# A two-block transformer kernel in split f32: weights one unit ahead, norm casts in pairs, transposes turned later, modulation steps spread

## The chip, the cores and the metric

The kernel runs on one core of one Trainium2 chip. The metric is the device time of one execution in microseconds (us); lower is better. TensorE is called PE here, VectorE DVE, ScalarE ACT, GpSimd POOL, and SyncE SP (the engine that issues the weight loads). Each engine runs its instructions in a fixed order; a scheduler sets that order when the program is built, and semaphores hold an instruction until its inputs are there.

## The reference, cut to what matters

256 tokens of width 1024 pass through a first block and then two layers of a second one. All is f32.

```python
def first_block(x, ...):                       # DEPTH = 1
    xn = rmsnorm(h, norm1_g); proj = xn @ w_in          # weights "wp"
    h = h + concat([moba_attention(...), hgrn2(...)]) @ w_out   # "wo"
    hn = rmsnorm(h, norm2_g)
    h = h + peer(hn, wq, subkeys, u, v)                  # "wq", "pu", "pv"
    return rmsnorm(h, normf_g)

def one(xb):                                   # peer: 16384 experts, 8 heads
    s = einsum(xb @ wq, subkeys)               # scores of two halves of a key
    v1, i1 = top_k(s[:, :, 0], 16); v2, i2 = top_k(s[:, :, 1], 16)
    sc, p = top_k(v1[..., :, None] + v2[..., None, :], 16)
    eidx = take_along_axis(i1 * 128 + i2, p)   # places of the chosen experts
    act = gelu(einsum(xb, u[eidx]))
    return einsum(softmax(sc) * act, v[eidx])

def even_layer(x, c, ...):                     # layer 0; layer 1 has attention instead
    sh_m, sc_m, g_m, sh_f, sc_f, g_f = split(silu(c) @ ada_w + ada_b, 6)
    h = modulate(rms_norm(x, mix_norm), sh_m, sc_m)
    y = mixer(h @ w_in) @ w_out                # "wi0", "wo0"   (layer 1: "wi1", "wo1")
    x = x + g_m * y
    hf = modulate(rms_norm(x, ffn_norm), sh_f, sc_f)
    return x + g_f * ((silu(hf @ w_gate) * (hf @ w_up)) @ w_down)   # "fgu", "fd"
```

## The kernel before, in words

**Products.** Every f32 product is done as three products of a high and a low part: hi by hi, hi by lo, lo by hi. The high part is a cast (on ACT), the low part a subtraction (on DVE). For weights these are `hi` (L193) and `lo` (L194); for a few units of "wq" and "pu" POOL does the subtraction. The matmuls are L224, L225 and L228 where the weights stand still in the array (128x256 results, "wq" and "pu" mainly), and L252, L253 and L254 where the activations stand still (128x512 results).

**The stream of weights.** All weights come in one order, in units of two halves; a half is 128x1024 f32, 512 KB, loaded into one of four `raw` buffers by SP and turned into `hi` and `lo` by ACT and DVE. There are three buffer pairs for `hi` and `lo`, and five more in the stretches where memory has room (`roomy`). `unit()` hands out a unit and first calls `load()` for those ahead of it: one unit, two where there is room. The place of a `load()` in the program sets where its cast and its subtraction stand in the orders of ACT and DVE.

**The norm.** `norm_t` runs before "wp", "wq", "wi0", "fgu0", "wi1" and "fgu1". For each half `t` of the tokens DVE forms the scale of the rows (L397 to `dr`, L409), PE turns the rows and scales them (L417, eight blocks of 128 columns), ACT scales each block (`y`, L420), casts four blocks at a time (`xh`, L424), DVE subtracts (`xl`, L425). Then PE starts the next product (`ahead`). The residual sum of the stage before is part of it (`gy` L744, `h` L745).

**PEER.** `places(t)` works out on DVE where each chosen expert lies (L876 to L878 per head group and half, results `res`), turns three tables on PE (L882) and copies them out (`idxT`, L883). `steps()` runs it in pieces beside the products with "pu"; `due` says beside which half. The tables are used by `gate4` (masks `A` L932 and `B` L933, product L935) from half 40 of "pu" on.

**Modulation.** `ada_steps` forms the six modulation vectors of a layer from 48 rows of `ada_w` (each 512 KB, `araw`): one DVE instruction per row (L1071), a sum at the end of a vector (L1075), and for the two gates a turn on PE (L1052), a copy on ACT (L1054) and a 4 KB store by SP (`send`). Layer 0's steps run beside "pv", layer 1's beside "fgu0" and "fd0".

**The feed-forward part.** `ffn` has 11 blocks of "fgu": 48 matmuls, then silu on ACT (L1110) and a product on DVE (`fy`, L1111), and a turn on PE (L1103) that is deferred into the next block, behind its k = 2.

Of the kernel before, what the change touches and what calls it, by code (L numbers as in the profile page):

```python
# [137 lines left out]
class Prog:  # L138
# [61 lines left out]
    def unit(self, nm, j):  # L200
        n = self.pos[(nm, j)]
        while self.nload < len(self.order) and self.nload <= n + (2 if self.roomy(self.nload) else 1):
            self.load(self.nload)
            self.nload += 1
        return self.ready.pop(n)
# [75 lines left out]
    def out_n512(self, nm, j0, x, first=None, step=None):  # L281

        us, acc = first or ([], [[self.acc([128, 512])], None])
        acc[1] = [self.acc([128, 512])]
        for k in range(8):
            if k // 4 == len(us):
                us.append(self.unit(nm, j0 + k // 4))
            o = (k % 2) * 512
            for t in (1,) if first else (0, 1):
                ins = self.xstat(acc, us[k // 4][k // 2 % 2], x, k, k == 0, k == 7, [(0, slice(o, o + 512))], ts=(t,))  # L290
            if k == 2:
                self.pump(ins)
            if step:
                step()
        return acc[0][0], acc[1][0]

    def ahead(self, nm, j0, x):

        us = [self.ready.pop(self.pos[(nm, j0 + n)]) for n in range(2)]
        acc = [[self.acc([128, 512])], None]  # L300
        for k in range(8):
            o = (k % 2) * 512
            ins = self.xstat(acc, us[k // 4][k // 2 % 2], x, k, k == 0, k == 7, [(0, slice(o, o + 512))], ts=(0,))
            if k == 5:
                self.mark = ins.ins
        return us, acc
# [65 lines left out]
    def norm_t(self, pool, side, nm, gain, shift=None, row=None):  # L372
# [7 lines left out]
        with self.tc.tile_pool(name="nrm", bufs=1, side=side) as tp:  # L380
            for t in range(2):
# [29 lines left out]
                for g in range(2):  # L411
# [6 lines left out]
                    for k in range(4):  # L418
# [3 lines left out]
                                             **({} if shift is None else {"bias": shift[:, c:c + 1]}))  # L422
                    xhs, xls = xh[:, 4 * g:4 * g + 4, ts], xl[:, 4 * g:4 * g + 4, ts]
                    c_ins = nc.scalar.copy(xhs, y)  # L424
                    v_ins = nc.vector.tensor_tensor(xls, y, xhs.bitcast(F32), op=ALU.subtract)  # L425
                if t == 0:
# [331 lines left out]
    JT = 40  # L758

    def peer(self):  # L760
# [8 lines left out]
        if True:  # L769
# [42 lines left out]
            def sums(t):  # L812


                cand = p2.tile([128, 8, 64], F32, name="cand", bufs=2)
                vv = v[t].rearrange("p (h two) k -> p h two k", two=2)
# [15 lines left out]
            def gains():  # L832
# [8 lines left out]
                for t in range(2):  # L841
# [3 lines left out]
                    nc.vector.tensor_tensor(gr[t], gr[t], sm[:, :, None].to_broadcast([128, 8, 16]), op=ALU.mult)  # L845

            def places(t):
                vi = p2.tile([128, 16, 16], F32, name="vi")
                ab = [p2.tile([128, 8, 16], F32, name=f"ab{n}") for n in range(2)]
                ai = p2.tile([128, 8, 16], U32, name="ai")  # L850
                res = [p2.tile([128, 8, 16], F32, name=f"res{n}") for n in range(2)] + [gr[t]]
                nc.vector.tensor_copy(vi, iu[t])
# [17 lines left out]
                for n in range(2):  # L870
                    for g in range(2):
# [6 lines left out]
                        nc.vector.tensor_reduce(res[n][:, hs], oh, axis=AX.X, op=ALU.add)  # L878
                        yield
                for n in range(3):  # L880
                    pt = self.acc([128, 128])
                    nc.tensor.transpose(pt, res[n].rearrange("p h k -> p (h k)"), self.ident)  # L882
                    nc.scalar.copy(idxT[n][:, t * 128:t * 128 + 128], pt)  # L883
                yield

# [76 lines left out]
            for j in range(JT // 2):  # L962
                u = self.unit("pu", j)
                for h in range(2):
                    experts(2 * j + h, u[h])
                    while n < len(due) and due[n] <= 2 * j + h:
                        next(st, None)
                        n += 1
# [20 lines left out]
            with tc.tile_pool(name="pv", bufs=1, side="right") as pr:  # L989
                acc = [[self.acc([128, 512]) for c in range(2)] for t in range(2)]  # L990
                self.silu_c(pr, self.sc, nc.vector, 2)
                nc.scalar.dma_start(self.gf, self.i["rows"][:, 0:1024].broadcast_to([128, 1024]))
                ada = self.ada_steps(pr, 0, 2, lambda: pg.tile([128, 128], F32, name="gr", tag="w", bufs=WB))
                tail = []
# [39 lines left out]
    def ada_steps(self, pool, l, bufs, small):  # L1034
# [13 lines left out]
        def send():  # L1048
            while due:
                g, m = due.pop(0)  # L1050
                pt = self.pt([8, 128])
                nc.tensor.matmul(pt, m, self.ident, start=True, stop=True)  # L1052
                r = small()[0:8]
                nc.scalar.copy(r, pt)  # L1054
# [7 lines left out]
        for n in range(6):  # L1062
# [19 lines left out]
            if n < 5:  # L1082
                yield
        send()
        yield


    def ffn(self, l, st=iter(()), final=False):
# [10 lines left out]
        def turn(b, ys):  # L1099
# [4 lines left out]
            self.split(yh[:, 2 * b:2 * b + 2], yl[:, 2 * b:2 * b + 2], pt)  # L1104

        for b in range(11):
            a01 = self.out_n512(f"fgu{l}", 2 * b, x, None if b else first)
            ys = [p.tile([128, 256], F32, name="fy", bufs=4) for t in range(2)]
# [3 lines left out]
            self.defer(lambda b=b, ys=ys: turn(b, ys))  # L1112
            if b:
                for _ in range(4 if b % 3 == 0 else 3):
                    next(st, None)
        acc = self.out_n(f"fd{l}", (yh, yl), 22, lambda: next(st, None))
# [10 lines left out]
    def even(self):  # L1127
# [7 lines left out]
        self.silu_c(pa, self.sc, nc.vector, 3)  # L1135
        st = self.ada_steps(pa, 1, 3, lambda: pa.tile([128, 128], F32, name="gr", bufs=1))
        p = es.enter_context(tc.tile_pool(name="ev", bufs=1))
# [257 lines left out]
```

## Time and profile before

| | |
|---|---|
| time, median of 3 runs | 1671.48 us (1671.35 to 1674.89) |
| the profiled execution | 1673.27 us, its span 1671.2 us |
| mean granted TensorE clock | 0.989 of full |
| busy: PE, DVE, ACT, POOL | 96%, 74%, 52%, 5% of the span |
| chain that ended last | PE 71%, DMA 11%, DVE 8%, ACT 5%, issue 4% |
| DMA | 323.00 MB, mean 193 GB/s |

The span is from the first to the last instruction; the time of an execution is a little longer. Busy time of PE is taken from modelled ends, so 96% doesn't say that PE is never held up: the waits view lists what held it. By stage, in us from the start of the span: "wp" and the first mixer to 152 or so with "wo" to 167, "wq" to 205, "pu" and "pv" to 1016, "wi0" to 1096, "wo0" to 1122, "fgu0" to 1265, "fd0" to 1332, "wi1" and "wo1" with attention between to 1470, "fgu1" to 1600, "fd1" to the end.

### The profile page before, as it was taken

The page shows a single profiled execution, that of the slowest core. Times are in us where ns is not written, and L with a number is a line of the kernel's source. Part 1 is how long each engine was busy: PE and PEld are TensorE (multiplying, and loading weights), DVE is VectorE, ACT ScalarE, POOL GpSimd, SP SyncE. Part 2 cuts the span into 40 slices and gives each one's busy share as a digit, 9 for nine tenths or more (in the row PEclk, how much of TensorE's full clock was granted, in tenths as well). Part 3 has the DMA queues.
Part 4 walks back from the last instruction along what each step waited for, and adds up shares of the span by engine and source line. Part 5 has one row for each costly group of instructions (what it writes and reads, how often), then busy time and mean ns, then how long its engine had stood idle before and what let it go on. Part 6 is the DMA issues. An engine that isn't in the chain of part 4 may idle for free.

```text
span 1671.2 us, 25969 instructions
## 1 busy us (share of the span) xinstructions
PE 1596.1 (96%) x9406; PEld 1397.1 (84%) x9406; DVE 1239.8 (74%) x2816; ACT 868.7 (52%) x1557; POOL 80.0 (5%) x47
## 2 busy tenths in 40 slices
PE   7899899999999999999999998999999899989998
PEld 6778799999999999888878886987787677768887
DVE  5896379948888898777777877986877678656553
ACT  6554555435444444555555555755434467755441
POOL 0120670000000000000000000000000000000000
PEclk9999999999999999999999999999999999999999
DMA  6433454534444444877778784765888653226552
GB/s 225 136 132 117 153 168 137 190 110 150 147 147 151 152 145 159 291 259 266 268 265 277 270 274 136 254 225 188 308 306 310 235 182 127 101 91 234 181 188 75
DMA packets 89041, 323.00 MB, mean 193 GB/s; under 512 B 9904, under 2 KB 10320, under 8 KB 88784
## 3 DMA queue, kind: packets, MB, share of 16 engines
q1 hardware_dynamic: 87904, 317.88, 56.3%
q10 hardware_dynamic: 1008, 3.47, 0.6%
q8 instruction: 73, 1.20, 0.3%
q14 instruction: 56, 0.46, 0.1%
HBM read 320.24 MB, written 1.06 MB: 192 GB/s over the span
## 4 chain that ended last, share of the span: by engine, by line
PE 71%; DMA 11%; DVE 8%; ACT 5%; issue 4%; POOL 1%; SPq 0%; ACTq 0%; DVEq 0%; POOLq 0%
PE acc L252 13%; PE acc L254 13%; PE acc L253 13%; PE pt L225 8%; PE pt L224 8%; PE pt L228 8%; DMA raw<-in_fgu 4%; PE acc L935 3%; DVE lo L194 3%; ACT hi L193 2%; DMA raw<-in_fd 2%; DVE araw L1071 2%; DMA raw<-in_wi 1%; ACT y L420 1%; DMA raw<-in_wp 1%
## 5 line engine op out<-in xcount | busy, mean ns | idle before, releaser
L194 DVE TENSOR_TENSOR lo<-raw,hi 128x1024 fp32r<-128x1024 f32 x476 | 579.2, 1223 | 265.7 <-ACT hi L193 258.2
L193 ACT CAST hi<-raw 128x1024 fp32r<-128x1024 f32 x500 | 523.9, 1051 | 449.9 <-PE acc L254 160.8
L224 PE MATMUL pt<-xh,hi 128*128 128x256 f32 x1344 | 338.6, 289 | 0.0
L225 PE MATMUL pt<-xl,hi 128*128 128x256 f32 x1344 | 332.5, 285 | 0.0
L225 PEld LDWEIGHTS pt<-xl,hi 128*128 128x128 f32 x1344 | 260.0, 193 | 0.3
L224 PEld LDWEIGHTS pt<-xh,hi 128*128 128x128 f32 x1344 | 259.8, 193 | 0.5 <-issue 0.2
L252 PE MATMUL acc<-hi,xh 128*128 128x512 f32 x544 | 218.1, 401 | 18.3 <-ACT xh L424 18.3
L254 PE MATMUL acc<-hi,xl 128*128 128x512 f32 x544 | 215.2, 396 | 0.7 <-DVE xl L425 0.7
L253 PE MATMUL acc<-lo,xh 128*128 128x512 f32 x544 | 213.8, 393 | 0.0
L252 PE MATMUL acc<-hi,wh 128*128 128x512 f32 x512 | 200.1, 391 | 1.7 <-ACT wh L326 1.7
L253 PE MATMUL acc<-lo,wh 128*128 128x512 f32 x512 | 199.9, 391 | 1.1 <-DVE lo L194 1.1
L254 PE MATMUL acc<-hi,wl 128*128 128x512 f32 x512 | 199.6, 391 | 1.5 <-DVE wl L327 1.5
L228 PE MATMUL pt<-xh,lo 128*128 128x256 f32 x1344 | 192.0, 285 | 0.0
L228 PEld LDWEIGHTS pt<-xh,lo 128*128 128x128 f32 x1344 | 174.1, 192 | 1.0 <-issue 0.8
L252 PEld LDWEIGHTS acc<-hi,xh 128*128 128x128 f32 x544 | 102.8, 189 | 41.9 <-ACT xh L424 20.6
L254 PEld LDWEIGHTS acc<-hi,xl 128*128 128x128 f32 x544 | 103.0, 189 | 27.4 <-DVE xl L425 5.7
L253 PEld LDWEIGHTS acc<-lo,xh 128*128 128x128 f32 x544 | 103.0, 189 | 19.9
L1071 DVE SCALAR_TENSOR_TENSOR araw<-araw,sc 128x1024 f32<-128x1024 f32 x96 | 116.1, 1219 | 0.1
L252 PEld LDWEIGHTS acc<-hi,wh 128*128 128x128 f32 x512 | 96.4, 188 | 23.2 <-ACT wh L326 3.1
L254 PEld LDWEIGHTS acc<-hi,wl 128*128 128x128 f32 x512 | 96.3, 188 | 22.6 <-DVE wl L327 2.8
L253 PEld LDWEIGHTS acc<-lo,wh 128*128 128x128 f32 x512 | 96.4, 188 | 21.2 <-DVE lo L194 1.5
L933 DVE TENSOR_SCALAR B<-iota,idxT,idxT 128x128 f32<-128x128 f32 x256 | 87.4, 341 | 0.0
(303 smaller groups left out, 1959.2 us busy)
## 6 DMA issues: line engine op xcount, KB each, us to landing
raw<-in_pu SPq DMA_DIRECT2D x128, 512.0 KB, 3.8
raw<-in_pv SPq DMA_DIRECT2D x128, 512.0 KB, 5.1
araw<-in_ada SPq DMA_DIRECT2D x96, 512.0 KB, 5.3
raw<-in_fgu SPq DMA_DIRECT2D x88, 512.0 KB, 5.2
raw<-in_wi SPq DMA_DIRECT2D x44, 512.0 KB, 5.0
raw<-in_fd SPq DMA_DIRECT2D x44, 512.0 KB, 5.0
raw<-in_wp SPq DMA_DIRECT2D x28, 512.0 KB, 5.7
raw<-in_wo SPq DMA_DIRECT2D x24, 512.0 KB, 4.6
```

Of the source, the lines that this page charges most:

```text
L193: nc.scalar.copy(hi, s)
L194: ins = eng.tensor_tensor(lo, s, hi.bitcast(F32), op=ALU.subtract)
L224: nc.tensor.matmul(out, hi[:, c], xh[:, k, ts], start=k == 0, stop=False)
L225: ins = nc.tensor.matmul(out, hi[:, c], xl[:, k, ts], start=False, stop=False)
L228: nc.tensor.matmul(out, lo[:, k * 128:k * 128 + 128], xh[:, k, ts], start=False, stop=k == K - 1)
L252: nc.tensor.matmul(a, xh, hi[:, cs], start=first, stop=False)
L253: nc.tensor.matmul(a, xh, lo[:, cs], start=False, stop=False)
L254: ins = nc.tensor.matmul(a, xl, hi[:, cs], start=False, stop=last)
L420: nc.scalar.activation(y[:, k], pt[:, k], AF.Copy if shift is None else AF.Identity, scale=gain[:, c:c + 1], **({} if shift is None else { ...
L933: nc.vector.tensor_scalar(B, iota, idxT[1][:, t:t + 1], idxT[2][:, t:t + 1], op0=ALU.is_equal, op1=ALU.mult)
L935: nc.tensor.matmul(gp[:, n], A, B, start=True, stop=True)
L1071: nc.vector.scalar_tensor_tensor(w, w, 1.0, self.sc, op0=ALU.mult, op1=ALU.mult, accum_out=m[:, k:k + 1])
```

## The change

Six edits, none of which changes what is computed:

1. `unit()` loads one unit ahead everywhere, and two only at the last unit of "wo", "pv" and "fd" streams (those that stand before a norm).
2. `norm_t` casts and subtracts two blocks at a time instead of four; `ahead` marks k = 3 instead of k = 5 (behind it the second half's L417 may be placed).
3. `places` no longer turns its tables; `turn(t)` for both halves is deferred to the first half of the last unit before the tables are used. `res` gets two buffers, `cand` one instead of two.
4. Modulation steps in `ffn` run between the k of a block (three in eight, and one more in every 24) instead of all behind the block.
5. `ffn` turns behind k = 4 instead of k = 2 (`self.at`).
6. The last gate's `send` is deferred to the next place that emits deferred work, and `gr` gets a buffer that lives long enough.

```diff
     def unit(self, nm, j):
         n = self.pos[(nm, j)]
-        while self.nload < len(self.order) and self.nload <= n + (2 if self.roomy(self.nload) else 1):
+        last = n + 2 < len(self.order) and self.order[n + 1][0] != nm and nm[0:2] in ("wo", "pv", "fd")
+        while self.nload < len(self.order) and self.nload <= n + (2 if last else 1):
...
-            if k == 2:
+            if k == self.at:
                 self.pump(ins)
...
+    at = 2
...
-            if k == 5:
+            if k == 3:
                 self.mark = ins.ins
...
-                    xhs, xls = xh[:, 4 * g:4 * g + 4, ts], xl[:, 4 * g:4 * g + 4, ts]
-                    c_ins = nc.scalar.copy(xhs, y)
-                    v_ins = nc.vector.tensor_tensor(xls, y, xhs.bitcast(F32), op=ALU.subtract)
+                        if k % 2:
+                            ks = slice(k - 1, k + 1)
+                            xhs, xls = xh[:, c - 1:c + 1, ts], xl[:, c - 1:c + 1, ts]
+                            c_ins = nc.scalar.copy(xhs, y[:, ks])
+                            v_ins = nc.vector.tensor_tensor(xls, y[:, ks], xhs.bitcast(F32), op=ALU.subtract)
...
-                cand = p2.tile([128, 8, 64], F32, name="cand", bufs=2)
+                cand = p2.tile([128, 8, 64], F32, name="cand", bufs=1)
...
-                res = [p2.tile([128, 8, 16], F32, name=f"res{n}") for n in range(2)] + [gr[t]]
+                res = [p2.tile([128, 8, 16], F32, name=f"res{n}", bufs=2) for n in range(2)] + [gr[t]]
...
+                done_res[t] = res
+
+            def turn(t):
                 for n in range(3):
                     pt = self.acc([128, 128])
-                    nc.tensor.transpose(pt, res[n].rearrange("p h k -> p (h k)"), self.ident)
+                    nc.tensor.transpose(pt, done_res[t][n].rearrange("p h k -> p (h k)"), self.ident)
                     nc.scalar.copy(idxT[n][:, t * 128:t * 128 + 128], pt)
-                yield
...
                 for h in range(2):
+                    if j == JT // 2 - 1 and h == 0:
+                        for t in range(2):
+                            self.defer(lambda t=t: turn(t))
                     experts(2 * j + h, u[h])
...
-        send()
+        self.defer(send)
...
+        self.at = 4
+        count = [0]
+
+        def step():
+            count[0] += 1
+            if count[0] % 8 in (2, 5, 7) or count[0] % 24 == 0:
+                next(st, None)
+
         for b in range(11):
-            a01 = self.out_n512(f"fgu{l}", 2 * b, x, None if b else first)
+            a01 = self.out_n512(f"fgu{l}", 2 * b, x, None if b else first, step if b else None)
...
-            if b:
-                for _ in range(4 if b % 3 == 0 else 3):
-                    next(st, None)
+        self.at = 2
```

In the new file lines stand a little lower: L420 becomes L424, L424 becomes L431, L882 becomes L894, L744 and L745 become L751 and L752.

The first place is ACT at the norm ahead of "fgu1". Of before, from the last square of the sums (`jk`, L443):

```order
L443 ACTIVATE jk,m_16140<-h_75 128x512
L420 ACTIVATE y<-pt,modc_85,modg_87 128x128 x5
L424 CAST xh<-y 128x4x128
L420 ACTIVATE y<-pt,modc_85,modg_87 128x128 x3
L443 ACTIVATE jk,m_16146<-h_75 128x512
L424 CAST xh<-y 128x4x128
L420 ACTIVATE y<-pt,modc_85,modg_87 128x128 x5
```

and of the change, the same place:

```order
L450 ACTIVATE jk,m_16184<-h_75 128x512
L424 ACTIVATE y<-pt,modc_85,modg_87 128x128 x3
L431 CAST xh<-y 128x2x128
L424 ACTIVATE y<-pt,modc_85,modg_87 128x128 x2
L431 CAST xh<-y 128x2x128
L424 ACTIVATE y<-pt,modc_85,modg_87 128x128 x2
L431 CAST xh<-y 128x2x128
L424 ACTIVATE y<-pt,modc_85,modg_87 128x128
L450 ACTIVATE jk,m_16190<-h_75 128x512
L431 CAST xh<-y 128x2x128
```

The first cast now stands behind three `y` instead of five, and is half as wide; there are four of them per half of the tokens instead of two. The orders at the norms ahead of "wq", "wi0", "fgu0" and "wi1" read alike.

The second place is PE in "pu". Of before, at the turn of the first half's tables, behind half 19 of "pu":

```order
L225 MATMUL pt<-xl,hi 128x256
L228 MATMUL pt<-xh,lo 128x256 x8
L882 MATMUL acc<-ident,res_2932 128x128
L882 MATMUL acc<-ident,res_2933 128x128
L882 MATMUL acc<-ident,gr_1773 128x128
L224 MATMUL pt<-xh,hi 128x256
L225 MATMUL pt<-xl,hi 128x256
```

and of the change, at the one place where all six tables are turned, at half 38 of "pu":

```order
L227 MATMUL pt<-xl,hi 128x256
L894 MATMUL acc<-ident,res_2936 128x128
L894 MATMUL acc<-ident,res_2937 128x128
L894 MATMUL acc<-ident,gr_1789 128x128
L894 MATMUL acc<-ident,res_3211 128x128
L230 MATMUL pt<-xh,lo 128x256 x7
L894 MATMUL acc<-ident,res_3212 128x128
L230 MATMUL pt<-xh,lo 128x256
L894 MATMUL acc<-ident,gr_1790 128x128
L226 MATMUL pt<-xh,hi 128x256
```

The first half's three turns are 19 halves of "pu" later in PE's order, the second half's nine.

The third place is DVE at the end of "wo0", where the residual sum and the norm ahead of "fgu0" begin. Of before:

```order
L327 TENSOR_TENSOR yl<-xr,yh 128x256
L194 TENSOR_TENSOR lo<-raw,hi 128x1024 x6
L744 TENSOR_TENSOR gy<-acc,g 128x512
L745 TENSOR_TENSOR h_74<-h_74,gy 128x512
L744 TENSOR_TENSOR gy<-acc,g 128x512
L745 TENSOR_TENSOR h_74<-h_74,gy 128x512
L397 SCALAR_TENSOR_TENSOR m<-m_13131,m_13137 128x1
```

and of the change:

```order
L331 TENSOR_TENSOR yl<-xr,yh 128x256
L194 TENSOR_TENSOR lo<-raw,hi 128x1024 x7
L751 TENSOR_TENSOR gy<-acc,g 128x512
L194 TENSOR_TENSOR lo<-raw,hi 128x1024
L752 TENSOR_TENSOR h_74<-h_74,gy 128x512
L751 TENSOR_TENSOR gy<-acc,g 128x512
L752 TENSOR_TENSOR h_74<-h_74,gy 128x512
L401 SCALAR_TENSOR_TENSOR m<-m_13155,m_13161 128x1
```

Eight `lo` instead of six stand behind the last `yl`, and the eighth is between the first `gy` and the first `h`. Away from these places the gate's turn L1052 leaves the end of "pv" for the first block of "wi0", and the end of "fd0" for the first block of "wi1"; its copy and its store move with it.

## Rows read from the trace of the kernel before

**Rows 1.** The page: busy us of each engine, share of the span, instructions.
```profile
PE 1596.1 (96%) x9406; PEld 1397.1 (84%) x9406; DVE 1239.8 (74%) x2816; ACT 868.7 (52%) x1557; POOL 80.0 (5%) x47
```

**Rows 2.** Waits of PE over the whole span: us, times, longest.
```profile
PE acc L252 <- ACT xh L424: 18.3, 12, 2.5
...
PE acc L882 <- DVE res L878: 7.0, 1, 7.0
PE pt L1052 <- DVE modc L1075: 6.1, 2, 3.5
PE pt L1103 <- DVE fy L1111: 5.2, 4, 1.9
PE acc L788 <- ACT qp L889: 4.5, 3, 2.6
...
PE acc L254 <- DVE wl L327: 1.5, 2, 1.2
```

**Rows 3.** Timeline of PE at the norm before "wi1": start, us, instruction, [idle before].
```profile
1336.20 0.50 PE L252 MATMUL acc<-hi,xh 128*128 128x512 f32 x1 [1.56 <-ACT xh L424]
...
1336.93 0.50 PE L254 MATMUL acc<-hi,xl 128*128 128x512 f32 x1
1337.26 0.39 PE L252 MATMUL acc<-hi,xh 128*128 128x512 f32 x1
...
1341.83 0.40 PE L254 MATMUL acc<-hi,xl 128*128 128x512 f32 x1
```

**Rows 4.** Timeline of ACT at the same norm.
```profile
1333.79 1.85 ACT L420 ACTIVATE y<-pt,modc,modg 128x128 f32<-128x128 f32 x5 [1.53 <-PE pt L417]
1335.52 0.63 ACT L424 CAST xh<-y 128x512 fp32r<-128x512 f32 x1
```

**Rows 5.** Timeline of ACT at the norm before "wq".
```profile
176.62 1.40 ACT L420 ACTIVATE y<-pt,cols 128x128 f32<-128x128 f32 x5 [0.31 <-PE pt L417]
```

**Rows 6.** Instructions on tile oh (attention): duration min/median/max in ns.
```profile
L1335 ACT CAST oh<-pt x8: 354/372/372, 1395.7 to 1464.9; 128x256 fp32r<-128x256 f32 x8
```

**Rows 7.** Timeline of PE at the turn of the first tables in "pu".
```profile
289.19 0.27 PE L882 MATMUL acc<-ident,res 128*128 128x128 f32 x1
296.48 0.44 PE L882 MATMUL acc<-ident,res 128*128 128x128 f32 x1 [7.02 <-DVE res L878]
```

**Rows 8.** Timeline of PE in "fd0" at the gate's turn.
```profile
1318.92 0.60 PE L1052 MATMUL pt<-ident,modc 128*8 128x128 f32 x2 [3.54 <-DVE modc L1075]
```

**Rows 9.** Windows behind both turns: us, busy of each engine, granted clock, DMA share, GB/s.
```profile
296.80:301.20 4.40, 4.40 (x22) 4.40 (x21) 3.13 (x9) 1.23 (x4) 0.00 (x0) 0.50 0.67 240
1319.40:1321.70 2.30, 2.30 (x6) 1.84 (x6) 1.14 (x2) 1.34 (x3) 0.00 (x0) 0.50 0.85 319
```

**Rows 10.** Timeline of DVE in "fgu0" behind a block.
```profile
1168.06 1.22 DVE L1071 SCALAR_TENSOR_TENSOR araw<-araw,sc 128x1024 f32<-128x1024 f32 x1
...
1171.50 0.75 DVE L1111 TENSOR_TENSOR fy<-fy,acc 128x256 f32<-128x256 f32 x2
```

**Rows 11.** Groups by line, 1122 to 1265 us ("fgu0"): count, busy us, mean ns, idle before.
```profile
L193 ACT CAST hi<-raw 128x1024 fp32r<-128x1024 f32 x43 | 44.9, 1049 | 60.2 <-DMA raw<-in_fgu 54.6 <-DVE araw L1071 3.8 <-DMA raw<-in_fd 1.2
```

**Rows 12.** Timeline of DVE at the end of "wo0".
```profile
1115.70 1.22 DVE L194 TENSOR_TENSOR lo<-raw,hi 128x1024 fp32r<-128x1024 f32 x1 [0.30 <-ACT hi L193]
1116.85 0.68 DVE L744 TENSOR_TENSOR gy<-acc,g 128x512 f32<-128x512 f32 x1
...
1123.17 0.29 DVE L409 TENSOR_SCALAR dr<-ident,r 128x128 f32<-128x128 f32 x1
```

**Rows 13.** Timeline of PE at the same place.
```profile
1123.52 1.72 PE L417 MATMUL pt<-dr,h 128*128 128x128 f32 x13 [1.26 <-DVE dr L409]
```

**Rows 14.** Timeline of POOL in "wq".
```profile
186.23 21.07 POOL L194 TENSOR_TENSOR lo<-raw,hi 128x1024 fp32r<-128x1024 f32 x9 [0.48 <-ACT hi L193]
```

More of the change, by code (lines that the diff above doesn't have):

```diff
@@ L845, in gains @@
                     nc.vector.tensor_tensor(gr[t], gr[t], sm[:, :, None].to_broadcast([128, 8, 16]), op=ALU.mult)
+            done_res = {}
             def places(t):
@@ L992, in peer @@
                 nc.scalar.dma_start(self.gf, self.i["rows"][:, 0:1024].broadcast_to([128, 1024]))
-                ada = self.ada_steps(pr, 0, 2, lambda: pg.tile([128, 128], F32, name="gr", tag="w", bufs=WB))
+                ada = self.ada_steps(pr, 0, 2, lambda g: pg.tile([128, 128], F32, name="gr", tag="w", bufs=WB) if g == 2
+                                     else self.rp.tile([128, 128], F32, name="gr", bufs=1))
                 tail = []
@@ L1052, in send @@
                 nc.tensor.matmul(pt, m, self.ident, start=True, stop=True)
-                r = small()[0:8]
+                r = small(g)[0:8]
                 nc.scalar.copy(r, pt)
@@ L1135, in even @@
         self.silu_c(pa, self.sc, nc.vector, 3)
-        st = self.ada_steps(pa, 1, 3, lambda: pa.tile([128, 128], F32, name="gr", bufs=1))
+        st = self.ada_steps(pa, 1, 3, lambda g: self.rp.tile([128, 128], F32, name="gr", bufs=1))
         p = es.enter_context(tc.tile_pool(name="ev", bufs=1))
```

## Prediction, made before the result was known

> **What bounds the kernel now.** I read the page first: PE is busy for 1596 us, DVE for 1240, ACT for 869 [rows 1]. PE has the most work by far, so the span is PE's work plus what holds PE up. The second view was therefore the waits of PE alone. Its rows are short and name the rest of the argument: the twelve half norms cost 18.3 us, one wait on `res` 7.0, the gates' turns 6.1, four waits on `fy` 5.2, three on `qp` 4.5, two on `wl` 1.5 [rows 2]. None of the six edits takes work from PE (the last gate's turn, the tables and `fy` are only turned elsewhere), so all that can be gained lies in these waits and in the slow clock behind two of them; all that can be lost is a new wait. The third view was the timeline at each of these places, the fourth the windows with the granted clock, the last the groups by line in "fgu0", where DMA, casts and modulation meet.
>
> **Norms, twelve halves.** The reader is to see that PE waits for one thing, the first cast of `xh` [rows 3], and that this cast stands behind five `y`, begun 1.73 us apart from it, 0.346 each, and itself takes 0.63 [rows 4]. In the change three `y` stand ahead and the cast is half as wide. No 128x256 cast of `y` is in the trace; the nearest one takes 0.37 [rows 6], and its bounds are 0.32 (half of 0.63) and 0.63. The first cast ends 2 x 0.346 + (0.63 - 0.37) = 0.95 us sooner. Ahead of "wp" and "wq" `y` has no bias and five take 1.40 with the last one's own length in it, some 0.25 apart [rows 5]: 2 x 0.25 + 0.26 = 0.76. The next pairs come every 2 x 0.346 + 0.37 = 1.06 us, and PE needs two blocks, six matmuls, of (1341.83 - 1337.26) / 20 = 0.229 each [rows 3], 1.37 us: the second cast is in time. Eight halves at 0.95 and four at 0.76 make 10.6. Against it: two more casts per half put (4 x 0.37 - 2 x 0.63) = 0.22 on ACT ahead of the weights' casts, and DVE has four subtractions instead of two between the second half's small steps, which PE covers with 24 matmuls. I take 10.3, with bounds of 6 (casts at 0.63) and 14 (the wait of 18.3 with what the first norm's casts of weights add, less what three `y` and a cast must take).
>
> The Trainium skill's page "VectorE: DVE Perf Modes", section "The TRN2 errata", speaks against this edit: each instruction with a source in SBUF pays a fixed latency, so tiles should be 512 wide or more. From its ScalarE formula I estimate 0.40 us for 256 columns, so 0.92 us saved instead of 0.95; by that the sum would lose 0.3 us. The row for 256 columns (0.37, over half of 0.63) agrees that a part is fixed.
>
> **Places.** PE stood from 289.19 to 296.48 because DVE's last reduction of the first tables came late, between subtractions of weights [rows 7]; it goes, since the turn is 19 halves of "pu" later: 7.3 less a 0.1 matmul pitch, 7.2. Behind it the granted clock was 0.50 for at least 4.4 us [rows 9], so 2.2 us were lost to the lower level, 1.2 GHz; that goes with the gap. What is late next: masks A and B can no longer be built before half 40, and ACT's six copies, then DVE's masks, stand before the first product L935. I charge 1 us (0 to 6: a wait as long as the old one is the upper bound). Together 8.4.
>
> **Scores in "wq".** The three waits on `qp` total 4.5 [rows 2]; `qp` stands in ACT's order behind casts, which wait for `raw` buffers, which POOL's subtractions free. One cast fewer stands ahead now. But POOL works without a break, 21.07 / 9 = 2.34 us per half [rows 14], and that pace stays. I take 2, bounds -1 and 4.5.
>
> **End of "pv".** The gate's turn leaves this place: of L1052's 6.1 us of waits the longest, 3.5, is in "fd0", so 2.6 is here [rows 2]. The waits on `wl`, 1.5, stay or grow, since DVE's order now puts a subtraction for "wi0" ahead of each `wl`, and those wait for loads: at one to three of them at 1.2 us, I take +2 for the place, bounds -1 and 6.
>
> **"fgu0".** Three modulation steps and an `fy` ran in a row [rows 10]; three steps at 1.14 apart are 3.4 us in front of `fy`. Now they stand between subtractions, and the turn comes two k later, 12 matmuls or 2.7 us. All four waits (5.2) should go. Two halves less of casts stand ahead of silu, and casts of this stretch wait 54.6 us for loads in 43 casts, 1.27 each [rows 11]: I charge one such wait. 4, bounds 0 and 7.
>
> **"fd0" and "wi1".** The turn's 3.5 us and half of 2.3 us at clock 0.50 go [rows 8, 9]: 4.7. In "wi1" the turn stands behind three matmuls of the first block; its vector has long been formed there. The copy takes its place on ACT behind the norm's casts, and the 4 KB store on SP behind loads; no one reads the row for a stage. Bounds 3.5 and 5. Behind this norm one turn of `q` is placed later: 0.7 more, 0 to 1.5.
>
> **"wo0" into the norm.** DVE is the path there, from the first `gy` to `dr`, and PE waits 1.26 for it [rows 12, 13]. A subtraction of 1.22 us now stands between `gy` and `h`: I charge 1.2, or 2.5 if its cast is late too, 0 if it is done before.
>
> **First units behind the norms.** With one unit less ahead, the first weights behind "wo0", "wi0" and "fgu1" have less in store: I charge 1.5 in all (0 to 8). In "pu" subtractions 14 to 19 come behind both head groups, covered by PE's 24 matmuls per result; nothing (0 to 3). One buffer for `cand` costs nothing, since one engine writes and reads it in order.
>
> **The sum.** 10.3 + 8.4 + 2 + 2 + 4 + 4.7 + 0.7 - 1.2 - 1.5 = 29.4, say 30 with the rounding of the clock. The profiled execution took 1673.3, which is 1.8 over the median; from it 1643.3, from the median of 1671.5 it is 1641.5. I forecast 1642, with 1634 to 1650 as the likeliest case's own range.
>
> **Rivals.**
> *The waits only move* (chance 0.21). For it: DVE and ACT execute in order, and the subtractions taken from before now stand beside `wl`, `gy` and `fy`; a shorter lead gives each less to draw on. Against it: PE has room at none of the removed waits, so the norms and "fd0" gain in any case. With "wq" and "pv" at -1 each, "fgu0" at 0, places at 3, the norms at 8, "fd0" at 4.7, "wo0" at -2.5: 10 us gained, up to 19; about 1657.
> *Everything at its upper end* (0.15). Norms 13, places 9.4, "wq" 4, "pv" 5, "fgu0" 6, "fd0" and "wi1" 6, "wo0" 0: 43 gained, 1628.
> *Weights too late in "fgu0"* (0.09): slower. Here 512 KB loads for weights and for modulation share SP's queue, and casts already wait for loads 1.27 us each. With two halves less in store (24 matmuls, 5.5 us), a load that lands late is no longer hidden. If all 40 halves behind the first block each came 1.27 us late, 51 us would be lost: 1642 + 51 = 1693, less some for steps that overlap. It decides from about 24 late halves. Against it: the four `raw` buffers stay, and the loads start when one falls free, which hardly hangs on the casts' order. The Trainium skill's page "Perfetto Trace Analysis", section "Optimization Strategy", reads gaps that repeat as a lack of buffers; by it less in store is the wrong way, and the time would be that of this rival. The trace shows gaps of that kind at four of eleven blocks only, and those waited for `fy`.
> *No change* (0.05): the places gain is eaten by late masks, the norms' by ACT, and the sum ends near 1671.
>
> **How the numbers follow.** 0.50 for the forecast, the rest as above. A difference of 0.2%, 3.3 us, is what a measurement of this kernel can tell from none. Faster 0.50 + 0.21 + 0.15 = 0.86, less 0.01 for a moved case that gains under 3.3; same 0.05, slower 0.10. The range holds the forecast, most of the moved waits and the better half of the upper case: 1626 to 1661.
>
> **What would show it.** Right: twelve waits on `xh` of some 0.6 us each, 8 in sum; no wait of L894 over 1 us and no clock of 0.50 near 296 and 1319; waits on `fy` under 1 us; the wait on `dr` ahead of "fgu0" near 2.5. Wrong: new rows of PE on `lo` in "fgu0", "wi0" or "wo0" above 5 us in all, on `wl` above 5, or on A or B at half 40 of "pu".

## The result, and the profile after

The changed kernel takes 1652.15 us (median of 4 runs, 1651.0 to 1652.82) against 1673.18 us of before in the same runs: a ratio of 0.9872, 95% interval 0.9854 to 0.989, so 21.4 us less (18 to 24). It was forecast at 1642 with a range of 1626 to 1661: faster, as forecast, inside the range, but with some two thirds of the 30 us forecast and outside the likeliest case's own range of 1634 to 1650. In a later comparison the same kernel stood at 0.984 (0.9815 to 0.9865), 27 us less (23 to 31), so the gain is known to be 18 to 31 us and no closer.

The page after, against [rows 1]:

```profile
span 1651.0 us, 25995 instructions
...
PE 1594.4 (97%) x9406; PEld 1396.9 (85%) x9406; DVE 1239.0 (75%) x2840; ACT 868.5 (53%) x1581; POOL 83.6 (5%) x47
```

PE, DVE and ACT are busy as long as before, though DVE and ACT have 24 instructions more each (the narrower casts and subtractions); the span is 20.2 us shorter. The waits of PE over the whole span, against [rows 2]:

```profile
PE pt L421 <- DVE dr L413: 17.5, 4, 8.3
PE acc L255 <- DVE lo L194: 7.1, 6, 2.0
PE acc L254 <- ACT xh L431: 6.1, 10, 0.9
PE acc L795 <- ACT qp L900: 4.1, 3, 2.7
...
PE acc L256 <- DVE wl L331: 2.2, 4, 1.1
```

and two more rows of before, which [rows 2] leaves out:

```profile
PE pt L417 <- DVE dr L409: 9.4, 2, 8.2
PE acc L253 <- DVE lo L194: 1.1, 1, 1.1
```

The rows on `res`, on `modc` and on `fy` behind a turn are gone, and the wait on `xh` is a third of what it was. In their place `lo` stands at 7.1 us in six waits (before one of 1.1), and `dr` at 17.5 in four (before 9.4 in two). One of the four on `dr`, 8.3 us, opens the kernel in both; the others are 1.5 us ahead of "wi0", 5.7 ahead of "fgu0" and 2.1 ahead of "wi1", where before had 1.3 ahead of "fgu0" and no other. So the waits that the edits aimed at went, all but a third of that on `xh`, and others came in at two names.

The starts of the six norms (the first L417, in the new file L421, of each in PE's timeline) cut the span in stages. In us:

| from the norm ahead of | "wp" | "wq" | "wi0" | "fgu0" | "wi1" | "fgu1" |
|---|---|---|---|---|---|---|
| stage, with the norm that opens it | "wp", "wo" | "wq", "pu", "pv" | "wi0", "wo0" | "fgu0", "fd0" | "wi1", "wo1" | "fgu1", "fd1" |
| before | 157.8 | 863.4 | 94.2 | 209.1 | 139.9 | 198.6 |
| after | 156.4 | 851.0 | 97.8 | 203.6 | 138.8 | 195.1 |
| difference | -1.4 | -12.4 | +3.6 | -5.5 | -1.1 | -3.5 |

The first stage is nearly the same program in all kernels and still lay between 151 and 160 us from one profiled execution to the next; a difference of 2 us there says nothing. In the trace of the second comparison, called the second execution from here on, the six differences are +1.3, -12.1, +1.1, -5.6, -1.5 and -1.5: the two large gains repeat, the rest moves by up to 3 us.

**The norm.** ACT at the norm ahead of "wi1", against [rows 4]:

```profile
1318.99 1.16 ACT L424 ACTIVATE y<-pt,modc,modg 128x128 f32<-128x128 f32 x3 [2.20 <-PE pt L421]
1320.04 0.40 ACT L431 CAST xh<-y 128x256 fp32r<-128x256 f32 x1
```

Three `y`, then a cast of 0.40 us, where five `y` and a cast of 0.63 stood. It starts 1.05 us behind the first `y` instead of 1.73.

**The end of "wo0".** DVE from the last subtractions to `dr`, against [rows 12]:

```profile
1103.97 1.23 DVE L194 TENSOR_TENSOR lo<-raw,hi 128x1024 fp32r<-128x1024 f32 x1 [1.84 <-ACT hi L193]
1105.11 0.69 DVE L751 TENSOR_TENSOR gy<-acc,g 128x512 f32<-128x512 f32 x1
1106.39 1.23 DVE L194 TENSOR_TENSOR lo<-raw,hi 128x1024 fp32r<-128x1024 f32 x1 [0.60 <-ACT hi L193]
1107.53 0.68 DVE L752 TENSOR_TENSOR h<-h,gy 128x512 f32<-128x512 f32 x1
...
1113.13 0.29 DVE L413 TENSOR_SCALAR dr<-ident,r 128x128 f32<-128x128 f32 x1
```

the cast it waits for on ACT, and PE's first matmul of the norm, against [rows 13]:

```profile
1105.31 1.05 ACT L193 CAST hi<-raw 128x1024 fp32r<-128x1024 f32 x1 [1.37 <-DMA raw<-in_fgu]
```

```profile
1113.47 0.80 PE L421 MATMUL pt<-dr,h 128*128 128x128 f32 x2 [5.71 <-DVE dr L413]
```

To be seen: both subtractions are late themselves, since their casts wait for loads; the residual sum waits behind them, and PE waits 5.71 us at the end of that row instead of 1.26. The 4.4 us more have two parts. From the first `gy` to `dr` it takes 8.0 us instead of 6.3, 1.7 more, for the subtraction in between and its own wait. And `gy` starts 2.7 us before PE's last matmul of "wo0" ends, where it was 5.4 before: 2.7 more.

**A modulation load ahead of a weight's load.** In "fgu0", SP's queue, the cast, and PE:

```profile
1170.16 0.39 SPq L178 DMA_DIRECT2D raw<-in_fgu  x1
1173.97 0.33 SPq L1057 DMA_DIRECT2D araw<-in_ada  x1
1174.39 1.33 SPq L178 DMA_DIRECT2D raw<-in_fgu  x3
```

```profile
1181.58 1.05 ACT L193 CAST hi<-raw 128x1024 fp32r<-128x1024 f32 x1 [3.64 <-DMA raw<-in_fgu]
```

```profile
1184.55 0.50 PE L255 MATMUL acc<-lo,xh 128*128 128x512 f32 x1 [1.31 <-DVE lo L194]
```

SP issues nothing from 1170.5 to 1174.0, then one modulation row and three halves of weights at once; the cast has to wait for the first of them, and PE for its subtraction. What SP waits for is the buffer of a modulation row, which a step on DVE (L1086, before L1071) frees; the view puts some of these waits down to `fy`, DVE's instruction beside the step. SP's waits ahead of these loads in the stage of "fgu0" and "fd0", of after and then of before:

```profile
SPq L1057 <- DVE araw L1086: 95.0, 34, 5.1
...
SPq L1057 <- DVE fy L1134: 4.3, 4, 1.1
```

```profile
SPq L1042 <- DVE araw L1071: 67.1, 29, 6.1
...
SPq L1042 <- DVE fy L1111: 25.3, 10, 6.5
```

Before, SP stood 92 us for them in all, after 99, so the shared queue is not new; but with the longer lead PE waited for no `lo` in "fgu0".

### The profile page after: what moved, and what is told of

It is laid out like the page before. It is cut to its first block, busy times and chain, and to the rows that moved or that the text cites. A ratio compares the mean times of both kernels' runs of the same rounds, so it can differ in the third digit from the quotient of the medians.

```text
span 1651.0 us, 25995 instructions
## 1 busy us (share of the span) xinstructions
PE 1594.4 (97%) x9406; PEld 1396.9 (85%) x9406; DVE 1239.0 (75%) x2840; ACT 868.5 (53%) x1581; POOL 83.6 (5%) x47
## 4 chain that ended last, share of the span: by engine, by line
PE 69%; DMA 13%; DVE 9%; ACT 5%; issue 3%; POOL 0%; SPq 0%; ACTq 0%; DVEq 0%; POOLq 0%
PE acc L254 13%; PE acc L256 13%; PE acc L255 13%; PE pt L230 7%; PE pt L226 7%; PE pt L227 7%; DMA raw<-in_fgu 4%; PE acc L946 3%; DVE lo L194 3%; ACT hi L193 3%; DMA raw<-in_wi 2%; DMA raw<-in_fd 2%; DVE araw L1086 2%; DMA raw<-in_wo 2%; DMA raw<-in_wp 1%
## 5 line engine op out<-in xcount | busy, mean ns | idle before, releaser
L1086 DVE SCALAR_TENSOR_TENSOR araw<-araw,sc 128x1024 f32<-128x1024 f32 x96 | 116.4, 1220 | 0.1
```

What stands on the lines that cost most here:

```text
L1086: nc.vector.scalar_tensor_tensor(w, w, 1.0, self.sc, op0=ALU.mult, op1=ALU.mult, accum_out=m[:, k:k + 1])
```

## The experiments

Ratios are to the kernel before on the same chip, with 95% intervals. On those chips the kernel before lay between 1669 and 1684 us; most of the intervals reach 0.002 to each side, 3.5 us. A gain over before in us is the ratio's. "The lead" is how many units of weights are loaded ahead.

Each edit alone was tried first, and the lead undone in the changed kernel.

**The lead undone.**

```diff
-        last = n + 2 < len(self.order) and ...
-        while ... and self.nload <= n + (2 if last else 1):
+        while ... and self.nload <= n + (2 if self.roomy(self.nload) else 1):
```

> The changed kernel with only the lead of the weights as before (two units ahead where there is room). Theory A, the shorter lead starves DVE of early subtractions: the changed kernel's waits on lo in fgu0 (about 5 us), at the start of wo0 (1.5) and the longer waits on dr at the ends of wo0 (4.4 longer than before) and fd0 (2.2) go, so 13 us less than the changed kernel: about 1639. Rival B, those waits come from the modulation steps now spread between the subtractions: the lead makes no difference, about 1652. Rival C, the shorter lead is itself a gain at wl, qp and fy: 1655 or more.

Measured: 1646.88 us, 0.9845 (0.9801 to 0.989). The interval holds the changed kernel's ratio, so the time does not tell the kernels apart. The waits of PE do:

```profile
PE pt L419 <- DVE dr L411: 15.7, 4, 8.1
...
PE acc L254 <- DVE wl L329: 4.2, 2, 3.6
```

No row on `lo` is left, as theory A said, and "fgu0" with "fd0" takes 200.7 us instead of 203.6; but PE waits on `dr` almost as long: 2.7 us instead of 5.7 at the end of "wo0", but 4.5 instead of 2.1 at the end of "fd0". `wl` (the low part of the activations that "pv" multiplies) at the end of "pv" waits 3.6, and the stage of "pu" and "pv" takes 854.0 instead of 851.0.

**The lead alone**, the same lines the other way round, in the kernel before.

> The kernel before with the shorter lead alone. Theory A: slower by about 13 us, 1685, with new waits on lo in fgu0 and a longer wait on dr at the end of wo0. Rival B: no difference, 1672. Rival C: faster by 3 to 5 us, 1668.

Measured: 1665.0 us, 0.994 (0.9919 to 0.9961), a gain of 10 us. Theory A falls here, as to the whole effect: the shorter lead is a gain by itself, more than rival C had. Waits of PE:

```profile
PE pt L419 <- DVE dr L411: 11.3, 2, 8.0
PE acc L254 <- ACT wh L328: 5.1, 3, 3.0
PE acc L884 <- DVE res L880: 4.7, 1, 4.7
...
PE pt L1105 <- DVE fy L1113: 1.0, 1, 1.0
```

`res` waits 4.7 instead of 7.0, `fy` behind the turns 1.0 instead of 5.2, and `modc` has no row: all three come sooner. In DVE's order fewer subtractions stand ahead of `res` and `modc`: 51 instead of 53 before the last reduction of the first tables, 280 instead of 283 and 377 instead of 379 before the vectors of the two gates. These are the waits that edits 3 to 6 take away as well. The lead has its price too: `wh`, the high part beside `wl`, waits 5.1 instead of 1.7, and `dr` at the end of "wo0" 3.2 instead of 1.3. "fgu0" with "fd0" takes 202.8 us with this edit alone and 203.6 with all six.

**The norm's casts alone** (edit 2, as in the diff above).

> The kernel before with the norm's casts of two blocks alone (and the mark at k = 3). Theory: PE's wait on xh falls from 18.3 us to about 6, the time by 12 us to about 1660. Rival, the wait moves to xl or to the second half's dr: gain under 6 us, 1667 or more.

Measured: 1667.4 us, 0.9951 (0.9931 to 0.9972), 8 us less. Waits of PE:

```profile
PE pt L1106 <- DVE fy L1114: 7.8, 7, 1.7
...
PE acc L252 <- ACT xh L427: 6.3, 11, 0.9
```

The wait on `xh` falls by 12 us as expected; the time falls by less, 5 to 12 us. `fy` is waited for seven times instead of four, 7.8 us instead of 5.2, but that can't be put down to this edit: with the deferred send alone (below), where DVE's order in "fgu0" is that of before, it was 7.7 in seven.

**The later turn of the tables alone** (edit 3).

> The kernel before with the later turn of the tables alone. Theory: the gap of 7.2 us and the 2.2 us at half clock behind it go, nothing comes in their place: 9.4 us less, about 1663. Rival, the tables come late for the masks at half 40: a new wait of 1 to 6 us there, 1665 to 1670.

Measured: 1669.36 us, 0.9965 (0.9944 to 0.9986), 6 us less (2 to 9). The row on `res` is gone; one new wait of 1.0 us stands on a copy of ACT:

```profile
PE pt L224 <- ACT actA L953: 1.0, 1, 1.0
```

That wait is at the lower end of what the rival has. The 8.4 us that the prediction took for the place lie within the interval.

**The modulation steps and the turn in "fgu" alone** (edits 4 and 5).

> The kernel before with the modulation steps spread over the blocks and the later turn alone. Theory: the four waits on fy (5.2 us) go, and with the lead of two units no wait on lo comes in their place: 5 us less than before, 0.997. Rival: waits on lo of 3 us or more as in the changed kernel, no gain.

Measured: 1668.99 us, 0.9956 (0.9939 to 0.9973), 7 us less. Two waits on `fy` are left, both at the last blocks, and no row on `lo`:

```profile
PE pt L1105 <- DVE fy L1121: 2.8, 2, 1.8
```

**The deferred send alone** (edit 6).

> The kernel before with the deferred send of the last gate alone. Theory: PE's waits on modc (6.1 us) and the slow clock behind them (about 2) go, but loads of the next stage set dr, so at the end of fd0 a wait on dr of 2 to 4 us comes in place of 5: 4 us less than before in all. Rival, nothing is given back: 8 us less.

Measured: 1677.73 us, 1.0008 (0.9992 to 1.0024): nothing, less even than the theory that had half given back. Waits of PE:

```profile
PE pt L417 <- DVE dr L409: 12.6, 3, 8.2
PE pt L1104 <- DVE fy L1112: 7.7, 7, 1.8
...
PE acc L254 <- DVE wl L327: 4.1, 2, 3.6
...
PE acc L252 <- DVE fy L1112: 3.3, 1, 3.3
```

The row on `modc`, 6.1 us, is gone, and each of its two places pays: at the end of "pv" `wl` now waits 3.6, and at the end of "fd0" `dr` has a new wait, 2.5 us. That makes 5 of the 6.1. The reading is that PE reaches the end of the stage sooner, but what stands ahead of `wl` and `dr` does not come sooner; no run here tests that for itself. `fy` waits more too (7.7 and 3.3 instead of 5.2 and 1.5), with DVE's order in "fgu0" as before: this differs between executions.

Then the changed kernel was run again and remedies were tried on it, one by one and together. **The changed kernel again:**

> The changed kernel itself, on the same chip as the next three, so that they can be compared with it: about 0.987 of the kernel before.

Measured: 1650.55 us, 0.984 (0.9815 to 0.9865). In its trace `lo` waits 5.2 us instead of 7.1, `dr` 4.9 at the end of "wo0" and 3.2 at the end of "fd0".

**The late subtractions.** Those of the second unit of "fgu0" and of "wi1" are held back and given to DVE behind `dr`; their casts stay:

```diff
                 nc.scalar.copy(hi, s)
+                if j == 1 and nm in ("fgu0", "wi1"):
+                    self.held.append((hi, lo, s))
+                    continue
                 ins = eng.tensor_tensor(lo, s, hi.bitcast(F32), op=ALU.subtract)
...
                 if t == 0:
+                    while self.held:
+                        hi, lo, raw = self.held.pop(0)
+                        with self.tc.issue_after(dr_ins):
+                            nc.vector.tensor_tensor(lo, raw, hi.bitcast(F32), op=ALU.subtract)
                     first = self.ahead(nm, 0, (xh, xl))
```

> The changed kernel with the two subtractions of the second unit of fgu0 and of wi1 given to DVE behind dr instead of ahead of the residual sum. Theory D, these subtractions wait for loads that land late and hold the residual sum and dr up: the waits on dr at the ends of wo0 (5.9 us in the changed kernel) and fd0 (2.2) fall to 1.5 and 0, 6 us less than the changed kernel. Rival, dr is late because of gy and h themselves or of PE's end: no difference, under 1 us. Rival, the subtractions are then late for the first product behind the norm: a new wait on lo of 1 to 3 us there.

Measured: 1644.31 us (1642.04 to 1644.68), 0.9806 (0.9784 to 0.9829), against 1650.55 (1646.44 to 1654.44) of the changed kernel: 6 us less. The intervals of the ratios overlap, but the runs themselves, on one chip, do not. It is theory D in size and place. Waits of PE, and DVE at the end of "wo0":

```profile
PE pt L425 <- DVE dr L417: 11.3, 4, 8.1
...
PE acc L259 <- DVE lo L199: 4.8, 5, 1.4
```

```profile
1099.38 0.68 DVE L759 TENSOR_TENSOR gy<-acc,g 128x512 f32<-128x512 f32 x1
1100.10 0.69 DVE L760 TENSOR_TENSOR h<-h,gy 128x512 f32<-128x512 f32 x1
...
1105.91 0.28 DVE L417 TENSOR_SCALAR dr<-ident,r 128x128 f32<-128x128 f32 x1
1106.11 2.35 DVE L441 TENSOR_TENSOR lo<-raw,hi 128x1024 fp32r<-128x1024 f32 x2
```

`gy` and `h` stand together, and the two subtractions stand behind `dr`, while PE and ACT work on the norm; the wait on `dr` falls from 17.5 (17.7 in the second execution) to 11.3: 0.5 is left at the end of "wo0" and 1.2 at the end of "fd0". No new wait on `lo` comes behind the norm. The stage of "wi0" and "wo0" takes 90.9 us, against 97.8 and 95.3 in the two executions of the changed kernel.

**Two units ahead for layer 0 alone.**

```diff
-        while ... and self.nload <= n + (2 if last else 1):
+        while ... and self.nload <= n + (2 if last or self.order[self.nload][0] in ("wi0", "wo0", "fgu0") else 1):
```

> The changed kernel with two units ahead again for wi0, wo0 and fgu0 alone. Theory A (the shorter lead is too short where DVE is busy with the mixer or the modulation): the waits on lo in wo0 (1.5) and fgu0 (5) go and dr at the end of wo0 waits 2.8 instead of 5.9: 9 us less than the changed kernel, less 2 to 4 of it given back by dr at the end of fd0. Rival B (the spread modulation steps make those waits): the waits on lo stay, 0 to 2 us less.

Measured: 1646.59 us, 0.9824 (0.98 to 0.9848), 4 us under the changed kernel, which the intervals don't part. Waits of PE:

```profile
PE pt L421 <- DVE dr L413: 15.0, 4, 8.2
...
PE acc L254 <- DVE fy L1134: 3.5, 1, 3.5
...
PE acc L255 <- DVE lo L194: 0.5, 1, 0.5
```

`lo` falls from 7.1 (5.2 in the second execution) to 0.5, and in "fgu0" to nothing, with the spread steps in place: the longer lead is enough to end it, against rival B. The start of "fd0" (`fy`, 3.5 instead of 1.7) and `dr` at its end (3.7) take some of it back.

**Both remedies.**

> The changed kernel with two units ahead for wi0, wo0 and fgu0 and the second unit's subtractions of fgu0 and wi1 behind dr. Theory: the two remedies take away different waits (lo in wo0 and fgu0, dr at the ends of wo0 and fd0), so 3 to 5 us less than with the late subtractions alone: ratio to the kernel before 0.977 to 0.979. Rival, loads set the pace of fgu0 and fd0 and what one remedy gains the start of fd0 gives back (a wait on fy of 3 us or more): 0.980 to 0.982.

Measured: 1641.13 us, 0.9787 (0.9765 to 0.9808), faster than both kernels: 36 us under before by this ratio, and its interval does not touch the changed kernel's. It does overlap that of the late subtractions alone (0.9806, 0.9784 to 0.9829), so that the second remedy adds to the first is not shown by the time. Waits of PE, in the fastest of its executions:

```profile
PE pt L425 <- DVE dr L417: 10.5, 3, 8.1
...
PE acc L259 <- DVE lo L199: 1.2, 2, 0.9
```

**The old lead everywhere, with the late subtractions.**

> The changed kernel with the old lead everywhere and the late subtractions. Theory: where PEER's tables and gates are already turned late, the shorter lead only helps wl at the end of pv (a wait of 3.7 us with the old lead) and qp; so 2 to 4 us slower than with both remedies. Rival, no difference to both remedies.

Measured: 1648.8 us, 0.9821 (0.9801 to 0.9841), 5.7 us slower than both remedies by the ratios, whose intervals touch; the runs themselves (1644.42 to 1649.63 against 1633.23 to 1644.0) do not. `wl` is at 4.3 us again. So some of the shorter lead is worth keeping. Where is less clear: of the difference between the two traces 2.0 us lie in the stage of "pu" and "pv", where `wl` is, and 5.2 in "fgu0" and "fd0", which the expectation did not name, and 7.4 in the first stage, which says nothing.

**The modulation rows on another queue.** POOL's queue loads them in "fgu0" and "fd0":

```diff
-                    nc.sync.dma_start(w, self.i[f"ada{l}"][fetch.n])
+                    (nc.gpsimd if l else nc.sync).dma_start(w, self.i[f"ada{l}"][fetch.n])
```

> The changed kernel with layer 1's modulation rows loaded by POOL's queue instead of SP's. Theory E, in fgu0 the weights' loads wait on SP behind loads of modulation rows, whose buffers the spread steps free late: with a queue of their own the weights' loads start when a raw buffer is free, the waits on lo in fgu0 (5 us in the changed kernel) fall to 1 or 2 and the time by 4 us. Rival A, the shorter lead alone makes them late: the waits stay. Rival F, DMA bandwidth is the bound in fgu0: the waits only move.

Measured: 1648.37 us, 0.9852 (0.9825 to 0.988), no difference to the changed kernel that can be measured. Waits of PE:

```profile
PE pt L1118 <- DVE fy L1134: 5.4, 4, 2.9
...
PE acc L255 <- DVE lo L194: 0.8, 1, 0.8
```

The waits on `lo` in "fgu0" go, as theory E has it, and with the short lead kept; but four waits on `fy` come in, 5.4 us. DVE's order there changes too, which may be why. Either remedy, the lead or the queue, ends the lateness of `lo`; whether bandwidth is the next bound (rival F) this run does not settle.

## Why the prediction was right in direction and too high in size

**Norms (10.3).** Right for the wait. A wait on `xh` fell from 18.3 / 12 = 1.53 to 6.1 / 10 = 0.61 us, 0.92 less where 0.95 and 0.76 were forecast; the cast takes 0.40 and not 0.37. Twelve make 11; alone the edit gave 8 us (5 to 12).

**Places (8.4).** Right: no wait on the turned tables, and the clock of 0.50 [rows 9] is gone. The window of that place after:

```profile
278.00:300.00 22.00, 22.00 (x184) 21.90 (x183) 22.00 (x30) 11.27 (x16) 0.00 (x0) 1.00 0.70 236
```

PE is busy throughout at a granted clock of 1.00. The charge of 1 us for late masks was not called for (0.3 on `actA`).

**"wq" (2).** Wrong: the wait on `qp` is 4.1 instead of 4.5. In the second execution it is 5.4. POOL works on without a break there, at the pace which the prediction named as what stays (2.34 us per half before, 30.51 / 13 = 2.35 after); that this pace is the whole cause, no run shows.

**"pv" (2), "fd0" (4.7).** The gates' waits went, but the run of this edit alone shows that they were not worth their 6.1 us: new waits of 5 us came in, on `wl` at the one place and on `dr` at the other. In the changed kernel, of the 2.6 us at the end of "pv", 0.7 is paid back on `wl` and 1.5 at a `dr` ahead of "wi0" that PE did not wait for before; the end of "fd0" pays back 2.1 (3.2 in the second execution) in the same way. No term of the sum held a wait on `dr` at these two places.

**"fgu0" (4).** The four waits on `fy` (5.2) went and 5 us of waits on `lo` came. The one late cast (1.27) charged was a quarter of it. The prediction's own sign of being wrong, new waits on `lo` above 5 us in "fgu0", "wi0" and "wo0", came true in the first execution (6.3) and just not in the second (4.5).

**"wo0" into the norm (-1.2) and first units (-1.5).** This is the step that failed most clearly. The prediction saw the subtraction between `gy` and `h`, priced it at its length, and gave 2.5 as its worst. It cost 4.4 us at `dr` (3.7 in the second execution): 1.7 between `gy` and `dr`, as charged and a little more, and 2.7 because the subtractions ahead of `gy` were late as well, which no term held. A wait of 1.3 on `lo` at the start of "wo0" came in the first execution alone. The late-subtractions run gives 6 us back by moving these and their like at "fd0" alone.

**The clock** was in no term but places and "fd0". TensorE is granted one of two levels, 1.2 GHz (0.50) or 2.4 GHz (1.00); a value between is the mean of a stretch. Behind the norm ahead of "fgu0", after the longer wait on `dr`, it was at the lower level:

```profile
1113.40:1118.00 4.60, 4.53 (x18) 4.30 (x19) 1.73 (x4) 2.41 (x8) 0.00 (x0) 0.50 0.32 129
```

With the late subtractions, where that wait is 0.5 us, the same stretch has 1.00:

```profile
1106.20:1110.80 4.60, 3.90 (x24) 3.28 (x25) 4.16 (x6) 3.35 (x11) 0.00 (x0) 1.00 0.46 153
```

There PE gets from the norm's first L421 to the 48th matmul of "fgu0" in 16.3 us; in the changed kernel it takes 18.2. So the lower level cost some 1.9 us, and no term held it. Behind the norm ahead of "fgu1" the clock was higher than before in the first execution and lower in the second. Windows of before, of after, and of the second execution:

```profile
1471.00:1491.00 20.00, 15.86 (x75) 13.06 (x76) 8.41 (x24) 11.76 (x28) 0.00 (x0) 0.91 0.07 27
```

```profile
1455.00:1475.00 20.00, 17.81 (x92) 14.92 (x93) 10.52 (x29) 14.42 (x33) 0.00 (x0) 1.00 0.16 52
```

```profile
1455.00:1475.00 20.00, 18.83 (x85) 16.09 (x86) 8.58 (x25) 12.79 (x32) 0.00 (x0) 0.84 0.11 35
```

So the last stage's gain of 3.5 us in the table owes something to the execution: 195.1 us at 1.00, 197.1 at 0.84. With the deferred send alone, whose norms are those of before, it took 198.2 at 1.00, so some 3 us are left where the clock is alike; and with the norm's casts alone it took 195.9, so most of the gain is theirs.

**The cost of the shorter lead** was put at 4 us (1.2, 1.5 and 1.3). The waits that go when the lead is undone come to some 9: 5.0 on `lo` in "fgu0", 1.3 at the start of "wo0", and 3.1 of the 5.7 on `dr` at its end. The wait on `dr` at the end of "fd0" is not among them; it grows to 4.5 with the lead undone, and is there with the deferred send alone (2.5). But waits are not time: with the lead undone the time was not measurably less, and `dr` there and `wl` took back some 4 us of what `lo` gave. By stage, the terms add up to some 10 us for "fgu0" with "fd0" (4, 4.7 and 1.9 for the two halves of the norm, less a part of the 1.5), of which 5.5 and 5.6 came in the two executions, and to about nothing for "wi0" with "wo0" (1.9 less 1.2 and another part), where 3.6 and 1.1 were lost. That is 8 of the 10 by which the first execution's 20.2 fall short of the sum, and 6 of the 11 or so of the second. The rival of late weights in "fgu0", 0.09, had the mechanism of the one; it named it as slower than before and so priced all 40 halves, where four waits came there (five in the second execution). The rival by which waits only move has the mechanism better than the forecast; in time the two comparisons, 21 and 27 us, lie between its 10 to 19 and the forecast's 30.

**What the prediction did not see at all** is that the edits cure the same waits. The lead alone takes 2.3 us off the wait on `res`, 4.2 off `fy` and all 6.1 off `modc`, and the later turns, the spread steps and the deferred send are there for the same three. Whether the gains in time are shared as well, the times don't settle: alone, the lead gives 10, the norm 8, places 6, the steps 7 and the send nothing, 31 us together, with some 7 us of uncertainty; in one kernel they give 21 or 27, each with 3 or 4 of its own. And which part of the gain the lead holds in the changed kernel stays open: undoing it changes the time by less than the comparison can tell.

## What to carry to other kernels

When several edits cure the same wait, price them as one, and look for the second cost of each where the cure is not needed. A wait that goes is worth only the distance to the next thing that is late at that place: before it is put in the sum, follow PE to the end of the stage and ask whether loads and the residual sum arrive sooner too. Work that prepares the next stage should stand in an in-order engine behind the chain that opens that stage, where there is room, and not ahead of it; here that was worth 6 us. And before a few us in one trace are explained, look at a second execution of the same kernel: the clock behind a norm changed between two executions of one program, and the waits on `fy` between kernels whose order on DVE is the same there.

## What the runs showed of the hardware

On one queue, loads of one kind held up loads of another through their buffers: SP issued nothing for 3.4 us while a modulation row waited for its buffer, and then, behind that row, three 512 KB halves within 1.3 us, the first of which was cast 7.2 us later; with the rows on POOL's queue PE's waits on `lo` were 0.8 us, against 7.1 and 5.2 in two executions of the changed kernel. Behind one norm of one program the granted clock was 1.00 over 20 us in one execution and 0.84 in another, and the stage took 195.1 and 197.1 us. And the same program differs by some us from one execution to the next: the first stage alone took 151 to 160 us in the fourteen traces.
